# The MLP of two token blocks by Strassen's seven products, with the inner units through DRAM

## The chip, the cores and the metric

The kernel runs on one core of a Trainium2 chip. The metric is the device time of one execution in microseconds (us), the median of several runs. Engines: TensorE (PE; its weight loads are PEld), VectorE (DVE), ScalarE (ACT), GpSimd (POOL), and SyncE (SP), whose queue issues every DMA of this kernel.

## The reference

`x` is 2048 tokens by 1024 channels, float32. A Conformer convolution module and a dense MLP each add to it:

```python
h = rms_norm(x, mix_norm)
a, g = split(h @ w_in + b_in)                # 1024 -> 2 x 1024
h = causal_depthwise_conv31(a * sigmoid(g)) + conv_b
x = x + (silu(layer_norm(h)) @ w_out + b_out)
x = x + square(relu(rms_norm(x, mlp_norm) @ mlp_w1)) @ mlp_w2   # 1024 -> 4096 -> 1024
```

## The kernel before

Channels lie on the 128 partitions and tokens along the free axis, so x comes in transposed and the result leaves transposed. The tokens are cut into four blocks of T = 512 columns, one PSUM bank each; channels into KD = 8 chunks of 128, hidden units into 32 chunks, taken in NG = 8 groups of G = 4.

A float32 product is made of three passes of float32r: each operand is split into `hi` (a ScalarE copy) and `lo` (a subtraction on VectorE or GpSimd) by `halves` (L84, L85), and hi*hi + hi*lo + lo*hi is accumulated in PSUM by `mm` (L143). So a 128x128 block of weights against 512 tokens is three matmuls, and every weight block and every moving tile is cast and subtracted once.

The program is written in Tile: the code gives the operations and the sizes of rotating buffers (`bufs`), and Tile puts in the waits. Each engine works through its own instructions in a fixed order. `spawn`, `poll` and `finish` weave a generator's steps (a norm) between the products: `mm` polls once per contraction step, and a task yields how many polls it waits (WAIT = 7 before a norm's first product, GAP = 9 before its second).

The order of the work: the first pointwise product and the gate for all blocks, with the depthwise convolution (31 steps of VectorE per chunk, L329) running beside the products of other blocks; blocks 0 and 1 are convolved and normalised on the chip, projected by `w_out` and taken through the MLP, while blocks 2 and 3 pass through DRAM (`spill`, `conv_out`) and are normalised by `ln_spilled`. Then, for blocks 2 and 3: `fetch` loads and splits the convolved tiles (`s`, `act`); `project` multiplies by `w_out`, adds the bias and x (L384) and collects squares for the norm; its `norm` scales and splits the result (L392, then `act`). `mlp` runs group 0 for block 2 alone and then for block 3 alone, and groups 1 to 7 for both. `mlp_up` makes four hidden chunks a group: 24 matmuls into a bank, relu (L407) and square (L409) on ScalarE, then a split into `hid`. `mlp_down` multiplies them by `w2` and adds each bank to the residual `x2`, kept in SBUF (L420); the last group's sums are stored to `outT`. Weights come as `raw` tiles of 128x1024 (two buffers) and are split into `w` (three). These last stages are:

```python
ss = [fetch(i) for i in range(2)]
a2, a, ta = project(2, ss[0])
b2, b, tb = project(3, ss[1])
finish(ta)
mlp(0, [2], [a2], [a], nc.gpsimd)
finish(tb)
mlp(0, [3], [b2], [b])
for g in range(1, NG):
    mlp(g, [2, 3], [a2, b2], [a, b])
```

## Time and profile before

| | |
|---|---|
| median of 3 runs | 1987.99 us (1987.82 to 1989.01) |
| profiled execution: span from the first to the last instruction | 1987.9 us |
| busy: TensorE, VectorE, ScalarE, GpSimd | 1955.0, 1369.3, 653.7, 373.9 us |
| matmuls | 8576 |
| of these 128x512, by moving tile and weights | 4800 `act` by `w`, 3456 `hid` by `w`, 192 `act` by `hid` |
| DMA | 190.83 MB, 96 GB/s over the span |

Busy time is the time in which an engine executes; an engine's row says nothing of why it is idle. The profiled execution gives no time outside its span, which is within 0.1 us of the median. Matmuls overlap their neighbours, so the mean of one (391 ns) is more than the step from one to the next.

### The profile page before, as it was taken

Reading aid. Unit: us, or ns where it says so; the run is one execution under the profiler, and the core shown is the slowest. Engines: PE = TensorE matmul, PEld = TensorE weight load, DVE = VectorE, ACT = ScalarE, POOL = GpSimd, SP = SyncE. Lnnn points to the kernel's source line nnn. Section 1 sums busy time; section 2 is a strip of 40 time slices with the busy share of each in tenths; the row PEclk is TensorE's granted clock in tenths of the full one; section 3 lists DMA queues with packets and bytes.
Section 4 is the critical chain, followed back from the end, with each engine's and each line's share of the span. In section 5 each row is a group of like instructions: output and inputs, shape, how many; then the busy total and the mean of one; then the engine's idle time right before and its main releaser. Section 6 shows DMA issues by size and latency. Waiting matters only on the chain.

```text
span 1987.9 us, 22177 instructions
## 1 busy us (share of the span) xinstructions
PE 1955.0 (98%) x8576; PEld 1606.3 (81%) x8576; DVE 1369.3 (69%) x1976; ACT 653.7 (33%) x960; POOL 373.9 (19%) x215
## 2 busy tenths in 40 slices
PE   7999999999999999999999999999999999999999
PEld 6888888888778878788888788878888888888887
DVE  7999999999999999789999863553223232322322
ACT  5223225243453333443222442433322313132230
POOL 2256322644445630000000002410000000000000
PEclk9999999999999999999999999999999999999999
DMA  6223321432224333552212484322111111111112
GB/s 199 64 85 111 98 77 65 143 102 96 85 81 130 124 107 117 194 183 96 66 66 72 142 276 153 118 85 85 43 53 43 53 50 46 53 43 53 43 53 85
DMA packets 69801, 190.83 MB, mean 96 GB/s; under 512 B 7872, under 2 KB 8000, under 8 KB 69696
## 3 DMA queue, kind: packets, MB, share of 16 engines
q1 hardware_dynamic: 69696, 189.43, 29.1%
q8 instruction: 67, 1.10, 0.2%
q14 instruction: 38, 0.31, 0.1%
HBM read 163.98 MB, written 25.41 MB: 95 GB/s over the span
## 4 chain that ended last, share of the span: by engine, by line
PE 55%; issue 3%; DVE 1%; ACT 1%; DMA 1%; POOL 0%; DVEq 0%; ACTq 0%
PE ps L143 54%; DMA conv<-s 1%; DVE xn L392 0%; DVE act L85 0%; ACT s L336 0%; PE lps L212 0%; DVE w L85 0%; ACT relu L407 0%; ACT sq L196 0%; POOL r L223 0%; ACT w L84 0%; PE lps L203 0%; POOL acc L192 0%; DVE c L364 0%; ACT hid L84 0%
## 5 line engine op out<-in xcount | busy, mean ns | idle before, releaser
L143 PE MATMUL ps<-act,w 128*128 128x512 f32 x4800 | 1104.6, 391 | 10.8 <-ACT w L84 8.4
L143 PEld LDWEIGHTS ps<-act,w 128*128 128x128 f32 x4800 | 902.5, 188 | 202.4 <-ACT w L84 8.4
L143 PE MATMUL ps<-hid,w 128*128 128x512 f32 x3456 | 799.6, 392 | 8.4 <-DVE hid L85 4.9
L143 PEld LDWEIGHTS ps<-hid,w 128*128 128x128 f32 x3456 | 650.8, 189 | 150.4 <-DVE hid L85 7.9
L84 ACT CAST w<-raw 128x1024 fp32r<-128x1024 f32 (+1 forms) x238 | 247.3, 1040 | 611.7 <-PE ps L143 579.3
L329 DVE SCALAR_TENSOR_TENSOR cacc<-hc,cw,cacc 128x512 f32<-128x512 f32 x464 | 324.6, 749 | 1.4
L420 DVE TENSOR_TENSOR h<-h,ps 128x512 f32<-128x512 f32 x256 | 174.6, 685 | 207.9 <-PE ps L143 205.8
L329 DVE SCALAR_TENSOR_TENSOR cacc<-h,cw,cacc 128x512 f32<-128x512 f32 x464 | 316.9, 749 | 0.0
L85 POOL TENSOR_TENSOR w<-raw,w 128x1024 fp32r<-128x1024 f32 x98 | 236.7, 2415 | 315.1 <-ACT w L84 300.0
L85 DVE TENSOR_TENSOR w<-raw,w 128x1024 fp32r<-128x1024 f32 (+1 forms) x140 | 171.0, 1223 | 170.5 <-ACT w L84 170.3
L407 ACT ACTIVATE relu<-ps 128x512 f32<-128x512 f32 x128 | 76.4, 597 | 370.8 <-PE ps L143 366.6
L85 DVE TENSOR_TENSOR hid<-s,hid 128x512 fp32r<-128x512 f32 x128 | 99.5, 778 | 127.5 <-ACT hid L84 127.2
L409 ACT ACTIVATE s<-relu 128x512 f32<-128x512 f32 x128 | 80.9, 632 | 1.2
L84 ACT CAST hid<-s 128x512 fp32r<-128x512 f32 x128 | 79.6, 622 | 3.7
L192 POOL TENSOR_TENSOR acc<-acc,hc 128x512 f32<-128x512 f32 x12 | 13.1, 1092 | 250.6 <-DVE hc L329 202.4
L192 POOL TENSOR_TENSOR acc<-acc,sq 128x512 f32<-128x512 f32 x36 | 50.1, 1391 | 37.7 <-ACT sq L196 37.0
L384 DVE SCALAR_TENSOR_TENSOR h<-ps,vec,xt 128x512 f32<-128x512 f32 x32 | 23.9, 748 | 42.5 <-PE ps L143 42.2
L303 ACT ACTIVATE sg<-ps,vec 128x512 f32<-128x512 f32 x24 | 16.5, 687 | 98.5 <-PE ps L143 98.5
L196 ACT ACTIVATE sq<-h 128x512 f32<-128x512 f32 x64 | 39.4, 626 | 19.5 <-DVE h L384 7.8
L143 PE MATMUL ps<-act,hid 128*128 128x512 f32 x192 | 45.0, 391 | 0.0
L143 PEld LDWEIGHTS ps<-act,hid 128*128 128x128 f32 x192 | 35.9, 188 | 7.4
L84 ACT CAST act<-xn 128x512 fp32r<-128x512 f32 x48 | 29.6, 621 | 36.6 <-DVE xn L392 23.5
(69 smaller groups left out, 558.4 us busy)
## 6 DMA issues: line engine op xcount, KB each, us to landing
raw<-in_w SPq DMA_DIRECT2D x176, 512.0 KB, 3.3
xt<-in_xT SPq DMA_DIRECT2D x64, 256.0 KB, 3.4
raw<-in_w_out SPq DMA_DIRECT2D x32, 512.0 KB, 3.9
raw<-in_w_in SPq DMA_DIRECT2D x30, 512.0 KB, 3.3
outT<-h SPq DMA_DIRECT2D x32, 256.0 KB, 2.9
spill<-hs SPq DMA_DIRECT2D x16, 271.0 KB, 2.3
hc<-spill SPq DMA_DIRECT2D x16, 271.0 KB, 2.8
h<-in_xT SPq DMA_DIRECT2D x16, 256.0 KB, 5.8
```

Of the source, the lines that this page charges most:

```text
L84: nc.scalar.copy(hl[:, 0, :], src)
L85: eng.tensor_sub(hl[:, 1, :], src, hl[:, 0, :].bitcast(F32))
L143: nc.tensor.matmul(ps, lhsT=w(k, a), rhs=x[:, b, :], start=k == 0 and i == 0, stop=k == len(xs) - 1 and i == 2,)
L192: eng.tensor_add(self.acc, self.acc, t)
L196: nc.scalar.activation(q, t, AF.Square)
L303: nc.scalar.activation(sg, pg, AF.Sigmoid, bias=v(V_BIN + KD + j))
L329: nc.vector.scalar_tensor_tensor(out, h[:, k : k + T], cw[:, j, k : k + 1], acc, ALU.mult, ALU.add)
L384: nc.vector.scalar_tensor_tensor(o, ps, v(V_BO + m), x_tile(m, b), ALU.add, ALU.add)
L407: nc.scalar.activation(r, ps, AF.Relu)
L409: nc.scalar.activation(s, r, AF.Square)
L420: nc.vector.tensor_add(x2[i][m], x2[i][m], ps)
```

## The change

The MLP of blocks 2 and 3 is computed as 2x2 block products by Strassen's algorithm in Winograd's form: seven products of half-sized blocks in place of eight, with sums of blocks before and after. Going up, the moving matrix is [B11 B12; B21 B22]: the columns are blocks 2 and 3, the rows the upper and lower four channel chunks. Its forms B11, B21, B22, T1 to T4 (four tiles each) are made once by `norm_first` and `norm_second`. A `Quad` is two hidden chunks for both blocks: `sums` makes S1 to S4 of its weights, seven products of 12 matmuls go to the banks x, y and z, some of them accumulating on one another after a copy of the bank was taken, and the four results are squared and kept. Their own forms (again B11, B21, B22, T1 to T4) are computed on GpSimd and stored to DRAM, `hid_d`. Going down, a unit is a group g of four hidden chunks and one half `o` of the output channels: `hidden` loads and splits the stored forms, `blocks` loads and combines `w2`, and each of the seven products is two tiles of 6 matmuls; the results are added to `acc`. The projected x goes to DRAM too (`x2d`) and is loaded for the norm and as the start of `acc`. The first EARLY = 5 quads do products P1 and P2 while block 3's norm is made, put them away in DRAM and resume. The tile pools of the first part are closed, and new ones lie over them; with `reuse_waits="tile"` a new tile waits for the old tiles under it. `w2` has another layout, so that `mlp_down` of blocks 0 and 1 loads it in runs of 256 columns. The core of the diff, blank lines left out:

```diff
+EARLY = 5
+N_WQ, N_LD, N_CC = 6, 5, 6
...
-    sb = pool("sb", bufs=1)
-    psp = pool("psp", bufs=5, space=PSUM)
-    psc = pool("psc", bufs=2, space=PSUM)
+    front = ctx.enter_context(ExitStack())
+    acts = sb = front.enter_context(tc.tile_pool(name="sb", bufs=1))
+    n_act, n_tmp = 2 * KD, 4
+    psp = front.enter_context(tc.tile_pool(name="psp", bufs=5, space=PSUM))
+    psc = front.enter_context(tc.tile_pool(name="psc", bufs=2, space=PSUM))
...
+    def load_w2(g, m, eng=nc.vector):
+        raw, hl = raw_w(), w_tile()
+        nc.sync.dma_start(raw.rearrange("p (s c) -> p s c", s=4), w2[g, m // 4][:, :, m // 2 % 2, :])
+        halves(hl, raw, eng)
+        def w(x, k, a):
+            at = (2 * x + k % 2) * 2 * P + k // 2 * P
+            return hl[:, a, at : at + P]
+        return w
...
-                w = load_w(w2[g, m // 2], eng)
+                w = load_w2(g, m, eng)
             for i, b in enumerate(blocks):
                 ps = bank()
-                mm(ps, lambda k, a: w(m % 2 * G + k, a), hid[i])
+                mm(ps, lambda k, a: w(m % 2, k, a), hid[i])
...
-    ss = [fetch(i) for i in range(2)]
-    a2, a, ta = project(2, ss[0])
-    b2, b, tb = project(3, ss[1])
+    front.close()
...
+    def reopened(name, stack, **k):
+        return stack.enter_context(tc.tile_pool(name=name, bufs=1, reuse_waits="tile", **k))
+    psp = reopened("psb", ctx, space=PSUM)
+    wts = reopened("wts", ctx)
+    forms = ctx.enter_context(ExitStack())
+    acts = reopened("acts", forms)
+    n_act, n_raw, n_tmp = 29, 2, 2
+    phase = ctx.enter_context(ExitStack())
+    sb = reopened("projection", phase)
+    def xbank():
+        return psp.tile([P, T], F32, name="px", tag="ps", bufs=3)
...
+    def w_split(src, eng):
+        hl = wts.tile([P, 2, T], F32R, name="wq", tag="wq", bufs=N_WQ)
+        nc.scalar.copy(hl[:, 0, :], src)
+        eng.tensor_sub(hl[:, 1, :], src, hl[:, 0, :].bitcast(F32))
+        return hl
+    def raw_wq(src):
+        t = sb.tile([P, 2 * T], F32, name="rawq", tag="rawq", bufs=n_raw)
+        nc.sync.dma_start(t, src)
+        return t
...
+    def product(ps, hl, xs, off=0, first=True):
+        n = len(xs)
+        for k, x in enumerate(xs):
+            for i, (a, b) in enumerate(((0, 0), (0, 1), (1, 0))):
+                nc.tensor.matmul(
+                    ps,
+                    lhsT=hl[:, a, off + k * P : off + (k + 1) * P],
+                    rhs=x[:, b, :],
+                    start=first and k == 0 and i == 0,
+                    stop=k == n - 1 and i == 2,
+                    skip_group_check=True,
+                )
+            poll()
...
+    def load_plain(src):
+        raw = raw_wq(src)
+        hl = [w_split(raw[:, h * T : (h + 1) * T], (nc.vector, nc.gpsimd)[h]) for h in range(2)]
+        return lambda k, a: hl[k // 4][:, a, k % 4 * P : (k % 4 + 1) * P]
+    def project_spilled(b, ss, norm):
+        st = Stats(False)
+        for m in range(KD):
+            w = load_plain(w_out[m])
+            ps = xbank()
+            mm(ps, w, ss)
+            xt = loaded(xT[m * P : (m + 1) * P, (b + 2) * T : (b + 3) * T], "xt")
+            o = out_tile()
+            nc.vector.scalar_tensor_tensor(o, ps, v(V_BO + m), xt, ALU.add, ALU.add)
+            nc.sync.dma_start(x2d[b][m], o)
+            st.add_square(m, o)
+        return spawn(norm(st))
+    def x_normed(b, m, rs, xn):
+        x = loaded(x2d[b][m], "x2")
+        nc.vector.scalar_tensor_tensor(xn, x, v(V_MLP + m), rs, ALU.mult, ALU.mult)
+        return xn
...
+    def norm_first(st):
+        rs = yield from st.rstd_later(WAIT, GAP)
+        for k in range(HK):
+            n0[k] = acts.tile([P, 2, T], F32, name="n0", tag="act", bufs=n_act)
+            for y in range(2):
+                form["B11" if y == 0 else "B21"][k] = act_split(x_normed(0, y * HK + k, rs, n0[k][:, y, :]))
+                yield 1
+    def norm_second(st):
+        rs = yield from st.rstd_later(WAIT, GAP)
+        for k in range(HK):
+            b12 = x_normed(1, k, rs, small(sb, "n1", 3))
+            b22 = x_normed(1, HK + k, rs, small(sb, "n1", 3))
+            b11, b21 = n0[k][:, 0, :], n0[k][:, 1, :]
+            t1 = small(sb, "t1", 1)
+            nc.vector.tensor_sub(t1, b12, b11)
+            t2 = small(sb, "t2", 1)
+            nc.vector.tensor_sub(t2, b22, t1)
+            form["T2"][k] = act_split(t2)
+            form["T1"][k] = act_split(t1, nc.gpsimd)
+            yield 1
+            nc.vector.tensor_sub(b12, b22, b12)
+            form["T3"][k] = act_split(b12)
+            form["B22"][k] = act_split(b22, nc.gpsimd)
+            nc.vector.tensor_sub(b21, b21, t2)
+            form["T4"][k] = act_split(b21)
+            yield 1
+    ss = [[act_split(loaded(conv_out[j][i], "s")) for j in range(KD)] for i in range(2)]
+    ta = project_spilled(0, ss[0], norm_first)
+    tb = project_spilled(1, ss[1], norm_second)
     finish(ta)
-    mlp(0, [2], [a2], [a], nc.gpsimd)
+    NQ = NF // 2
+    hid_d = [{n: dram.tile([P, T], F32, name=f"h{n}_{q}") for n in form} for q in range(NQ)]
+    def added(ps, t, out=None):
+        out = out_tile() if out is None else out
+        nc.vector.tensor_add(out, ps, t)
+        return out
+    def squared_relu(c, src=None):
+        nc.scalar.activation(c, c if src is None else src, AF.Relu)
+        nc.scalar.activation(c, c, AF.Square)
+        return c
+    class Quad:
+        def __init__(self, q):
+            self.q, self.early = q, False
+        def keep(self, n, t):
+            nc.sync.dma_start(hid_d[self.q][n], t)
+        def high(self):
+            self.a1 = raw_wq(w1[2 * self.q])
+            self.x = xbank()
+        def sums(self):
+            a2 = raw_wq(w1[2 * self.q + 1])
+            a11, a12, a21, self.a22 = self.a1[:, :T], self.a1[:, T:], a2[:, :T], a2[:, T:]
+            self.s1, self.s2 = small(sb, "s1", 1), small(sb, "s2", 1)
+            nc.vector.tensor_add(self.s1, a21, self.a22)
+            nc.vector.tensor_sub(self.s2, self.s1, a11)
+            nc.vector.tensor_sub(a21, a11, a21)
+            self.s3, self.s4 = a21, a12
+        def p1(self):
+            product(self.x, w_split(self.a1[:, :T], nc.vector), form["B11"])
+            self.c1 = small(wts, "p1", 2)
+            nc.scalar.copy(self.c1, self.x)
+        def p2(self):
+            y = ybank()
+            product(y, w_split(self.a1[:, T:], nc.vector), form["B21"])
+            self.c11 = squared_relu(added(y, self.c1))
+            self.keep("B11", self.c11)
+        def leave(self):
+            self.early = dram.tile([P, T], F32, name=f"p1_{self.q}")
+            nc.sync.dma_start(self.early, self.c1)
+        def resume(self):
+            self.high()
+            self.c1 = small(wts, "p1", 2)
+            nc.sync.dma_start(self.c1, self.early)
+            self.c11 = out_tile()
+            nc.sync.dma_start(self.c11, hid_d[self.q]["B11"])
+        def copied(self, ps, name):
+            t = small(sb, name, 2)
+            if self.early:
+                return added(ps, self.c1, t)
+            nc.scalar.copy(t, ps)
+            return t
+        def p6(self):
+            product(self.x, w_split(self.s2, nc.vector), form["T2"], first=bool(self.early))
+            self.u2 = self.copied(self.x, "u2")
+            nc.vector.tensor_sub(self.s4, self.s4, self.s2)
+        def p5(self):
+            self.z = zbank()
+            product(self.z, w_split(self.s1, nc.vector), form["T1"])
+            self.c5 = self.copied(self.z, "p5")
+        def p7(self):
+            product(self.x, w_split(self.s3, nc.vector), form["T3"], first=False)
+            self.c22 = squared_relu(added(self.x, self.c5))
+            self.keep("B22", self.c22)
+        def p3(self):
+            product(self.z, w_split(self.s4, nc.gpsimd), form["B22"], first=False)
+            self.c12 = squared_relu(added(self.z, self.u2))
+        def p4(self):
+            product(self.x, w_split(self.a22, nc.gpsimd), form["T4"], first=False)
+            if self.early:
+                c21 = squared_relu(added(self.x, self.c1))
+            else:
+                c21 = squared_relu(out_tile(), self.x)
+            self.keep("B21", c21)
+            c11, c12, c22 = self.c11, self.c12, self.c22
+            t1, t2, t4 = [small(sb, n, 1) for n in ("h1", "h2", "h4")]
+            nc.gpsimd.tensor_sub(t1, c12, c11)
+            nc.gpsimd.tensor_sub(t2, c22, t1)
+            nc.gpsimd.tensor_sub(c12, c22, c12)
+            nc.gpsimd.tensor_sub(t4, c21, t2)
+            for n, t in (("T1", t1), ("T2", t2), ("T3", c12), ("T4", t4)):
+                self.keep(n, t)
+    quads = [Quad(q) for q in range(NQ)]
+    for u in quads[:EARLY]:
+        u.high()
+        u.p1()
+        u.p2()
+        u.leave()
     finish(tb)
-    mlp(0, [3], [b2], [b])
-    for g in range(1, NG):
-        mlp(g, [2, 3], [a2, b2], [a, b])
+    phase.close()
+    sb, n_raw = reopened("first", phase), 4
+    last = None
+    for u in quads:
+        if u.early:
+            u.resume()
+            u.sums()
+        else:
+            u.high()
+            u.sums()
+            u.p1()
+        if last:
+            last.p3()
+        if not u.early:
+            u.p2()
+        u.p6()
+        if last:
+            last.p4()
+        u.p5()
+        u.p7()
+        last = u
+    last.p3()
+    last.p4()
+    phase.close()
+    sb = reopened("second", phase)
+    ORDER = (("A11", "B11"), ("A12", "B21"), ("S2", "T2"), ("S1", "T1"), ("S3", "T3"), ("S4", "B22"), ("A22", "T4"))
...
+    def hidden(g):
+        out = {}
+        for n in (b for _, b in ORDER):
+            out[n] = [act_split(loaded(hid_d[2 * g + k][n])) for k in range(2)]
+        return out
+    def blocks(g, o):
+        a11, a12, a21, a22 = [small(sb, "w2r", 8) for _ in range(4)]
+        for i, t in enumerate((a11, a12, a21, a22)):
+            nc.sync.dma_start(t.rearrange("p (q c) -> p q c", q=2), w2[g, o][:, i])
+        s1, s2 = small(sb, "s1", 1), small(sb, "s2", 1)
+        nc.gpsimd.tensor_add(s1, a21, a22)
+        nc.gpsimd.tensor_sub(s2, s1, a11)
+        out = {"A11": w_split(a11, nc.vector), "A12": w_split(a12, nc.vector)}
+        out["S2"] = w_split(s2, nc.vector)
+        out["S1"] = w_split(s1, nc.vector)
+        nc.vector.tensor_sub(a21, a11, a21)
+        out["S3"] = w_split(a21, nc.vector)
+        nc.vector.tensor_sub(a12, a12, s2)
+        out["S4"] = w_split(a12, nc.vector)
+        out["A22"] = w_split(a22, nc.gpsimd)
+        return out
+    def both(tiles, name, hs, w, first=True):
+        for i, ps in enumerate(tiles):
+            product(ps, w, hs, off=i * 2 * P, first=first)
+    h = hidden(0)
+    for g in range(NG):
+        for o in range(2):
+            if g == 0:
+                for b in range(2):
+                    for m in range(4 * o, 4 * o + 4, 2):
+                        t = acts.tile([P, 2, T], F32, name="acc", tag="act", bufs=n_act)
+                        for i in range(2):
+                            acc[b][m + i] = t[:, i, :]
+                            nc.sync.dma_start(acc[b][m + i], x2d[b][m + i])
+            ws = blocks(g, o)
+            px, py, pz = [[f() for _ in range(2)] for f in (xbank, ybank, zbank)]
+            both(px, "P1", h["B11"], ws["A11"])
+            p1 = [copied(t, "p1", wts) for t in px]
+            both(py, "P2", h["B21"], ws["A12"])
+            c = [added(t, p) for t, p in zip(py, p1)]
+            def add(x, n, ts):
+                for i, t in enumerate(ts):
+                    a = acc[n][4 * o + 2 * i + x]
+                    nc.gpsimd.tensor_add(a, a, t)
+            add(0, 0, c)
+            both(px, "P6", h["T2"], ws["S2"], first=False)
+            u2 = [copied(t, "u2") for t in px]
+            both(pz, "P5", h["T1"], ws["S1"])
+            p5 = [copied(t, "p5") for t in pz]
+            both(px, "P7", h["T3"], ws["S3"], first=False)
+            add(1, 1, [added(t, p) for t, p in zip(px, p5)])
+            both(pz, "P3", h["B22"], ws["S4"], first=False)
+            add(0, 1, [added(t, p) for t, p in zip(pz, u2)])
+            both(px, "P4", h["T4"], ws["A22"], first=False)
+            for i, t in enumerate(px):
+                a = acc[0][4 * o + 2 * i + 1]
+                nc.vector.tensor_add(a, a, t)
+            if g == NG - 1:
+                for m in range(4 * o, 4 * o + 4):
+                    for b in range(2):
+                        nc.sync.dma_start(outT[m * P : (m + 1) * P, (b + 2) * T : (b + 3) * T], acc[b][m])
+            if o == 0 and g < NG - 1:
+                nxt = hidden(g + 1)
+        h = nxt
...
-        "w2": _tiles(a["mlp_w2"][0], G, 2),
+        "w2": np.ascontiguousarray(
+            a["mlp_w2"][0].reshape(NG, 2, 2, P, 2, 2, 2, P).transpose(0, 4, 3, 6, 2, 5, 1, 7)
+        ).reshape(NG, 2, P, 4, 2, 2 * P),
```

## Rows read from the trace of the kernel before

**Rows 1.** The page's table of engines: busy us, share of the span, instructions.
```profile
PE 1955.0 (98%) x8576; PEld 1606.3 (81%) x8576; DVE 1369.3 (69%) x1976; ACT 653.7 (33%) x960; POOL 373.9 (19%) x215
```

**Rows 2.** The chain that ended last, from 1280 us: start us, us, what.
```profile
1308.61 674.99 PE ps L143 x2963
...
1983.62 0.69 DVE h L420
```

**Rows 3.** Stretches: length, each engine's busy us (instructions), TensorE's clock, DMA share, GB/s.
```profile
1190.00:1234.00 44.00, 44.00 (x196) 36.44 (x195) 15.87 (x17) 12.22 (x16) 10.48 (x6) 1.00 0.54 172
...
1279.00:1308.00 29.00, 26.06 (x119) 21.31 (x117) 20.41 (x30) 14.70 (x24) 11.87 (x6) 1.00 0.25 84
1308.00:1374.00 66.00, 65.39 (x275) 53.53 (x276) 28.23 (x31) 20.67 (x28) 4.77 (x2) 0.95 0.29 96
...
1374.00:1940.00 566.00, 566.00 (x2499) 468.67 (x2498) 166.93 (x204) 150.79 (x217) 0.00 (x0) 1.00 0.15 49
```

**Rows 4.** Groups from 1374 to 1940 us: busy us, mean ns, idle before, releaser.
```profile
L420 DVE TENSOR_TENSOR h<-h,ps 128x512 f32<-128x512 f32 x97 | 66.7, 687 | 151.9 <-PE ps L143 151.9
...
L85 DVE TENSOR_TENSOR hid<-s,hid 128x512 fp32r<-128x512 f32 x55 | 38.1, 693 | 118.3 <-ACT hid L84 118.3
L409 ACT ACTIVATE s<-relu 128x512 f32<-128x512 f32 x55 | 34.8, 632 | 0.9
L84 ACT CAST hid<-s 128x512 fp32r<-128x512 f32 x55 | 34.3, 623 | 1.8
L407 ACT ACTIVATE relu<-ps 128x512 f32<-128x512 f32 x55 | 32.9, 598 | 183.0 <-PE ps L143 183.0
```

**Rows 5.** Timeline, two runs of three VectorE sums: start us, us, what.
```profile
1186.54 1.88 DVE L420 TENSOR_TENSOR h<-h,ps 128x512 f32<-128x512 f32 x3
...
1303.17 1.88 DVE L85 TENSOR_TENSOR act<-xn,act 128x512 fp32r<-128x512 f32 x3
```

**Rows 6.** GpSimd instructions on `act` and `acc`: duration ns min/median/max.
```profile
L85 POOL TENSOR_TENSOR act<-xn,act x8: 1302/1745/1752, 188.8 to 203.0; 128x512 fp32r<-128x512 f32 x8
...
L192 POOL TENSOR_TENSOR acc<-acc,sq x36: 1281/1295/2152, 86.3 to 1282.5; 128x512 f32<-128x512 f32 x36
```

**Rows 7.** Timeline from 188 to 201 us, GpSimd, then VectorE.
```profile
188.76 6.86 POOL L85 TENSOR_TENSOR act<-xn,act 128x512 fp32r<-128x512 f32 x4 [7.06 <-ACT act L84]
...
188.61 2.44 DVE L272 SCALAR_TENSOR_TENSOR xn<-xt,vec,rstd 128x512 f32<-128x512 f32 x2
190.97 0.74 DVE L329 SCALAR_TENSOR_TENSOR cacc<-h,cw,cacc 128x512 f32<-128x512 f32 x1
...
193.34 2.82 DVE L272 SCALAR_TENSOR_TENSOR xn<-xt,vec,rstd 128x512 f32<-128x512 f32 x2
```

**Rows 8.** DMA: SP's issues of `s` (ns min/median/max), then us to landing.
```profile
L163 SPq DMA_DIRECT2D s<-conv x16: 319/382/496, 848.2 to 1180.4; - x16
...
raw<-in_w SPq DMA_DIRECT2D x176, 512.0 KB, 3.3
...
outT<-h SPq DMA_DIRECT2D x32, 256.0 KB, 2.9
...
s<-conv SPq DMA_DIRECT2D x16, 256.0 KB, 4.4
```

**Rows 9.** Timeline from 1278 to 1312 us: the norm of block 3.
```profile
1278.93 0.75 DVE L384 SCALAR_TENSOR_TENSOR h<-ps,vec,xt 128x512 f32<-128x512 f32 x1 [4.69 <-PE ps L143]
...
1292.88 3.17 DVE L392 SCALAR_TENSOR_TENSOR xn<-h,vec,rstd 128x512 f32<-128x512 f32 x2 [1.69 <-ACT rstd L242]
...
1306.40 1.36 DVE L85 TENSOR_TENSOR act<-xn,act 128x512 fp32r<-128x512 f32 x2
...
1308.61 3.78 PE L143 MATMUL ps<-hid,w 128*128 128x512 f32 x8 [3.55 <-ACT hid L84]
```

**Rows 10.** Timeline from 1184 us: last split and first matmul of the projections.
```profile
1184.19 0.69 DVE L85 TENSOR_TENSOR act<-s,act 128x512 fp32r<-128x512 f32 x1 [1.70 <-ACT act L84]
...
1190.15 2.20 PE L143 MATMUL ps<-act,w 128*128 128x512 f32 x9
```

More of the change, by code (lines that the diff above doesn't have):

```diff
@@ L87, in act_tile @@
     def act_tile():
-        return sb.tile([P, 2, T], F32R, name="act", tag="act", bufs=2 * KD)
+        return acts.tile([P, 2, T], F32R, name="act", tag="act", bufs=n_act)
     def hid_tile():
@@ L370, in ln_spilled @@
             nc.sync.dma_start(conv_out[j][i], s)
-    def fetch(i):
-        return [act_split(stream("s", conv_out[j][i])) for j in range(KD)]
     def project(b, ss, eng=nc.vector):
@@ new lines, in conformer_mlp, with ybank, zbank @@
+    forms = ctx.enter_context(ExitStack())
[5 more added lines that the diff above has]
+        return psp.tile([P, T], F32, name="px", tag="ps", bufs=3)
+    def ybank():
+        return psp.tile([P, T], F32, name="py", tag="py", bufs=2)
+    def zbank():
+        return psp.tile([P, T], F32, name="pz", tag="pz", bufs=2)
+    def w_split(src, eng):
[3 more added lines that the diff above has]
+        return hl
@@ new lines, in conformer_mlp @@
+    x2d = [[dram.tile([P, T], F32, name=f"x2_{b}_{m}") for m in range(KD)] for b in range(2)]
+    def load_plain(src):
[14 more added lines that the diff above has]
+        return spawn(norm(st))
@@ new lines, in x_normed @@
+    def x_normed(b, m, rs, xn):
+        x = loaded(x2d[b][m], "x2")
+        nc.vector.scalar_tensor_tensor(xn, x, v(V_MLP + m), rs, ALU.mult, ALU.mult)
+        return xn
+    HK = KD // 2
+    form = {n: [None] * HK for n in ("B11", "B21", "B22", "T1", "T2", "T3", "T4")}
+    n0 = [None] * HK
+    def norm_first(st):
[5 more added lines that the diff above has]
+                yield 1
@@ new lines, in conformer_mlp, with copied @@
+    last.p3()
[3 more added lines that the diff above has]
+    ORDER = (("A11", "B11"), ("A12", "B21"), ("S2", "T2"), ("S1", "T1"), ("S3", "T3"), ("S4", "B22"), ("A22", "T4"))
+    acc = [[None] * KD for _ in range(2)]
+    def copied(ps, name, pool_=None):
+        t = small(pool_ or sb, name, 2)
+        nc.scalar.copy(t, ps)
+        return t
+    def hidden(g):
[3 more added lines that the diff above has]
+        return out
```

10 lines of the change are left out of this document (9 added, 1 removed).

## The prediction, before the changed kernel was run

> **What bounds the kernel now.** The page's table of engines comes first [rows 1]: TensorE is busy 98% of the span, VectorE 69%, ScalarE 33%, GpSimd 19%. An average over unlike stages decides little, so the next view is the chain of waits [rows 2]: from 1308.61 us to the end it is one piece of 674.99 us of matmuls, and after it a last sum on VectorE. The table by stretches [rows 3] then shows what stands beside the matmuls. From 1374 to 1940, thirteen of the alternating up and down halves of the MLP of blocks 2 and 3, TensorE is busy 566.00 of 566.00 us at a granted clock of 1.00 (its 2.4 GHz level), VectorE 166.93, GpSimd nothing. So in the part that is changed, TensorE alone sets the time, VectorE has some 70% to spare, and a matmul costs 566.00 / 2499 = 0.2265 us.
>
> **Removed.** Up, before: 32 hidden chunks x 8 channel chunks x 3 passes x 2 blocks = 1536 matmuls; down: 8 groups x 8 x 4 x 3 x 2 = 1536. After: 16 quads x 7 products x 4 chunks x 3 = 1344, and 16 units (8 groups x 2 values of `o`) x 7 x 2 tiles x 2 chunks x 3 = 1344. That is 384 fewer, of the same 128x512 shape and passes: 384 x 0.2265 = **-87.0 us**. A quad or a unit is 84 matmuls, 19.0 us. The Trainium skill (TensorE: Matmul & The Clock Gate, Back-to-back issue gap) gives 512 / 2.4 + 2.5 = 216 ns; by it the gain would be an estimated 83 us. The trace says 226.5 ns, and that decides.
>
> **Prices of what is added.** A VectorE sum over 512 columns lasts about 0.69 us in the table of groups [rows 4], but three in a row take 1.88 us, with one operand in PSUM as with both in SBUF [rows 5]: each next one costs (1.88 - 0.69) / 2 = 0.60 us. A ScalarE cast or copy is 0.62, relu 0.60, square 0.63 [rows 4]. A GpSimd sum or split is 1.30 alone (the lowest of `act`, `acc`) and up to 1.75 [rows 6]. Why, the timeline shows [rows 7]: between 188.76 and 195.62 four GpSimd splits take 6.86 us, 1.72 each, while VectorE's `xn` instructions, which read two tensors in SBUF, take 2.44 and 2.82 us for two; the convolution step at 190.97, with its other tensor in PSUM, takes its usual 0.74. GpSimd and a VectorE instruction with two SBUF inputs exclude each other; GpSimd holds VectorE up for about 1.72 - 0.66 = 1.05 us each. An instruction with an operand in PSUM goes on beside it.
>
> **The up half, per quad (19.0 us of TensorE).** VectorE: 3 in `sums`, 5 splits, 1 in `p6` (nine with two SBUF inputs) and 3 sums out of PSUM: 12 x 0.60 = 7.2 us. GpSimd: 2 splits and 4 sums of hidden units, 6 x 1.05 = 6.3. Even end to end that is 13.5. ScalarE: 7 casts, 3 copies, 8 for the squared relu, 18 x 0.62 = 11.2. DMA: two loads of 512 KB and seven stores of 256 KB, at some 0.35 us of SP's queue each [rows 8], 3 us; 2.8 MB in 19 us is 150 GB/s, where 172 GB/s went beside full matmuls [rows 3]. Each bank that a later product accumulates on must first be copied; two other products, 5.4 us, stand between. TensorE hides all of it; I put **+3 us** for 16 quads (0 to 16, a microsecond each).
>
> **The down half, per unit (19.0 us).** VectorE: 6 splits, 2 differences, 7 splits of hidden units (14 tiles a group, two units): 15 with two SBUF inputs, 9.0 us; 8 sums out of PSUM, 4.8. GpSimd: s1, s2, the split of A22, 6 sums into `acc`: 9 x 1.05 = 9.5. None of VectorE's 13.8 or GpSimd's 9.5 is above 19.0, but on the shared access to SBUF they add up: 9.0 + 9.5 = 18.5, nearly a unit, and if no GpSimd instruction finds VectorE at a PSUM sum, VectorE needs 13.8 + 9.5 = 23.3. So the ends are 19.0 (hidden) and 23.3. PSUM sums come in pairs, and the first one's GpSimd sum can run beside the second: 3 x 0.60 = 1.8 saved, some 0.8 more by chance, against 0.3 of waiting for casts and matmuls: I take 21.0, between the ends. What a held split delays is queued behind it on VectorE: the sums out of `px` after P7, which P4 must have before it accumulates on the same banks, three banks of 6 matmuls or some 4 us later; so short holds cost nothing and only the total counts. **16 x 2.0 = +32 us** (0 to 69). ScalarE (14 casts, 6 copies, 12.4 us) and DMA (5.7 MB a group of 38 us) have room.
>
> **The norm of block 3.** Before, its statistics come 14.0 us after the last projection product (1278.93 to 1292.88) and its 16 VectorE instructions run until 1307.8; TensorE then waits 3.55 us for a hidden unit [rows 9]. In 95 us there [rows 3] 394 matmuls ran where 419 fit: 5.7 us lost, 3.3 of them by the clock of 0.95 over 66 us after the wait. After, the same moment needs per chunk pair 2 normalised tiles (0.66 each) and 7 sums or splits on VectorE (5.5 us), and 2 GpSimd splits (2.1): 4 x 7.6 = 30.5 us, nearly serial, as `t1` and `t2` have one buffer. What covers it are the five early quads, 120 matmuls, 27.2 us. T2's last chunk comes some 4.7 us before the end: 14.0 + 30.5 - 4.7 = 39.8. TensorE can do 9 of P6's 12 matmuls before (2.0): it stands 10.6 us, and pays 3.3 for the clock. Less the 5.7 of before, **+8 us** (-6 if all is covered, +18 if `s2`, which lies where older statistics lay, waits for the end of the norm).
>
> **Seams and ends.** The new pools lie over old tiles. Before, blocks 2 and 3 have their inputs split 5 us ahead of their first matmul (1184.88 against 1190.15) [rows 10]; after, some of these tiles may lie over x2 of block 1, which is free only when its result is stored, 2.9 us after the last sum [rows 8], and then need a cast and a split, 1.2: **+3** (0 to 8). From up to down, a weight block must land (about 4.4, as `s` [rows 8]), be cast and split, but most of its room is free a quad earlier: **+3** (0 to 8). x2 and the hidden units' passage through DRAM is loads of this kind, ordered well ahead; no more for it. `w2` of blocks 0 and 1 comes in runs of 1 KB: a load lands in 3.3 us now [rows 8] and even at 5 two raw buffers give one each 4 us, under the 5.4 of 24 matmuls: 0. At the end two more stores queue: **+1.5** (0 to 3).
>
> **Sum.** -87.0 + 3 + 32 + 8 + 3 + 3 + 1.5 = -36.5. Against the profiled span of 1987.9 us (the runs' median is 1987.99, so nothing to add) that is **1951 us**. No measurement of this kernel tells less than about 0.2%, 4 us, from no change.
>
> **Rivals.** (a) *TensorE stays the bound in the down half*: the PSUM sums fall beside GpSimd's, 19.0 a unit, and the 32 us vanish: 1919 us. For it: VectorE at 13.8 of 19.0; against it: 18.5 of 19.0 of the shared access, in strict order. The Trainium skill (Perfetto Trace Analysis, Identifying the Most-Contended Engine) says that the engine with the highest occupancy limits a regime. By that rule TensorE limits and this case holds; rows 7 show a resource that no engine's occupancy counts.
> (b) *VectorE and GpSimd set the down half*: fully serial, 23.3, and TensorE, held at a bank whose sum is queued behind GpSimd, then lets VectorE wait six matmuls (1.4 us) once a unit: 24.7, 16 x 5.7 = 91 us, so 2010 us, slower. It decides from (87.0 - 18.5) / 16 = 4.3 above 19.0, at 23.3 a unit. For it: two buffers of `py` and `pz`, three of `px`, so little slack; against it: some overlap is certain, since sums into `acc` follow pairs.
> (c) *The passage through DRAM and the three reopened pools hold TensorE*: SP's one queue keeps loads behind stores that wait for GpSimd, a microsecond for each quad (+13 over the 3) and the upper ends at the seams and the norm (+20): 1984 us, no change. Against it: loads run a quad ahead.
> That the matmuls don't fall is excluded by the count.
>
> **Chances.** Forecast, 1930 to 1975: 0.48; (a) 0.26; (b) 0.14; (c) 0.12, half of it on the faster side. Faster 0.80, same 0.06, slower 0.14. The range of 1914 to 2000 takes in (a) and (c) and leaves out (b) and some below (a), under 2 in 10.
>
> **What would show it.** 8192 matmuls. Up quads at 19.0 us each with VectorE near half busy; down units at 21 us, VectorE over 85% busy, its two-SBUF splits well above their 0.69 us, GpSimd's sums at 1.7, TensorE waiting for sums out of PSUM in `px`. A gap near 11 us after the early quads. If down units run at 19.0, the exclusion was sized wrongly, (a); if up quads exceed 20, the order of the queues, (c). Wrong altogether if TensorE's step per matmul changes with groups of 6 or 12.

## The result, and the profile after

The changed kernel takes 2001.86 us (median of 4 runs, 2000.47 to 2002.29) where the kernel before took 1987.9: the ratio is 1.0071, with a 95% interval of 1.0056 to 1.0085. It is slower, by 14 us or 0.7%, where 37 us less was forecast, and it lies just above the range. The profiled execution has a span of 1999.6 us, 11.7 above that of before. Its own time is 2001.76, so 2.2 us lie outside the span; in every run here these are 1.7 to 2.2, the kernel before included (1986.61 us with a span of 1984.8). So that its profiled span equals its median suggests that the profiled execution was some 2 us longer than the median one. The account below is of the 11.7 us between the two spans.

The page's table of engines of the changed kernel (busy us, share of the span, instructions), which answers to [rows 1]:

```profile
PE 1883.3 (94%) x8192; PEld 1538.8 (77%) x8192; DVE 1640.7 (82%) x2315; ACT 820.4 (41%) x1322; POOL 751.3 (38%) x471
```

The 384 matmuls are gone and TensorE is busy 72 us less; so it must be idle longer. The table by stretches of the changed kernel, to be read beside [rows 3] (length, then each engine's busy us and instructions, granted clock, DMA share, GB/s), shows where:

```profile
1210.00:1304.00 94.00, 93.57 (x405) 77.24 (x406) 42.57 (x65) 37.78 (x63) 40.55 (x31) 0.97 0.66 223
1304.00:1355.00 51.00, 28.81 (x121) 23.09 (x119) 38.91 (x57) 22.68 (x41) 15.33 (x10) 0.81 0.40 136
1355.00:1420.00 65.00, 59.96 (x244) 48.56 (x245) 41.82 (x59) 26.00 (x44) 28.65 (x20) 0.91 0.57 194
1420.00:1640.00 220.00, 217.92 (x961) 180.14 (x960) 132.83 (x146) 122.13 (x218) 105.53 (x72) 1.00 0.48 159
1640.00:1670.00 30.00, 15.87 (x51) 12.22 (x51) 11.01 (x16) 13.21 (x24) 9.96 (x7) 0.67 0.76 257
1670.00:1950.00 280.00, 260.80 (x1127) 211.18 (x1126) 256.95 (x308) 152.48 (x267) 191.25 (x121) 0.99 0.46 144
```

The steady part of the up half (1420 to 1640) is full. Two short stretches are half empty: the norm of block 3 (1304 to 1355) and the passage from up to down (from 1640). In these two stretches the granted clock averages 0.81 and 0.67, a mix of the 1.2 and the 2.4 GHz level. The down half is 7% empty. What TensorE waits for, from 1180 us on (us in total, times, longest):

```profile
PE px L586 <- ACT wq L561: 24.9, 2, 14.1
PE px L163 <- ACT wq L561: 22.8, 1, 22.8
PE px L586 <- DVE acc L864: 18.7, 14, 2.9
PE py L586 <- DVE cc L665: 13.7, 1, 13.7
```

Four long waits make 61.4 us: 22.8 ahead of the projections, 13.7 and 10.8 in the norm, 14.1 ahead of the down half. The 14 short ones are the down half's. They stand behind the last VectorE sums of a unit, those after P4 (L864), which free the `px` banks for the next unit. The prediction had expected waits for sums out of `px`, but for those after P7, inside the unit.

**Where the time went.** With 0.2265 us a matmul, by the starts of the stages in the timelines:

| stretch | lost or saved, us |
|---|---|
| first projection product at 1210.43, before at 1190.15 | +20.3 |
| projections, 1210.43 to 1301.69, for 384 matmuls | +4.3 |
| early quads, norm, up half, seam: 1301.69 to 1660.52, 1344 matmuls | +54.4 |
| down half, 1660.52 to 1994.78, 1344 matmuls | +29.9 |
| after the last product: 4.8, before 4.3 | +0.5 |
| lost in these places before: 1190.15 to 1983.62, less 3456 matmuls | -10.7 |
| 384 matmuls | -87.0 |
| sum | +11.7 |

**The front seam.** The timeline of the changed kernel, SP's issues and the first weights:

```profile
1161.76 26.92 SPq L439 DMA_DIRECT2D outT<-h  x11
...
1188.72 14.63 SPq L575 DMA_DIRECT2D s<-conv  x16
1203.41 0.42 SPq L567 DMA_DIRECT2D rawq<-in_w_out  x1
...
1209.76 1.14 ACT L561 CAST wq<-rawq 128x512 fp32r<-128x512 f32 x2 [2.18 <-DMA rawq<-in_w_out]
...
1210.43 5.87 PE L163 MATMUL px<-act,wq 128*128 128x512 f32 x13 [22.84 <-ACT wq L561]
```

SP works through its issues in order. Until 1188.7 it stands at the last eleven stores of blocks 0 and 1, which wait for VectorE's sums (ten waits, 22.5 us); then sixteen `s` loads pass through five buffers at the pace of the splits (eleven waits, 6.8 us); only then come the first weights. Before, `s` was issued by 1180.4 [rows 8] and split by 1184.88 [rows 10], while TensorE was still at the last products of blocks 0 and 1.

**The norm of block 3.** Its timeline, the second product of early quad 2, VectorE's `t1` of the later chunk pairs, the sum of that early quad, what TensorE does behind it, and quad 0's weights:

```profile
1315.59 1.42 DVE L618 SCALAR_TENSOR_TENSOR n<-x,vec,rstd 128x512 f32<-128x512 f32 x2 [0.52 <-ACT rstd L262]
...
1316.75 2.88 PE L586 MATMUL py<-act,wq 128*128 128x512 f32 x12
...
1322.31 1.78 DVE L641 TENSOR_TENSOR t<-n,n 128x512 f32<-128x512 f32 x1
...
1330.03 1.75 DVE L641 TENSOR_TENSOR t<-n,n 128x512 f32<-128x512 f32 x1
...
1337.70 1.74 DVE L641 TENSOR_TENSOR t<-n,n 128x512 f32<-128x512 f32 x1
...
1340.64 0.68 DVE L665 TENSOR_TENSOR cc<-py,p 128x512 f32<-128x512 f32 x1
...
1341.46 5.02 PE L586 MATMUL py<-act,wq 128*128 128x512 f32 x12 [13.66 <-DVE cc L665]
...
1350.39 0.87 SPq L567 DMA_DIRECT2D rawq<-in_w  x2
...
1355.15 0.69 DVE L690 TENSOR_TENSOR s<-rawq 128x512 f32<-128x512 f32 x1 [6.67 <-DMA rawq<-in_w]
...
1357.27 3.23 PE L586 MATMUL px<-act,wq 128*128 128x512 f32 x6 [10.80 <-ACT wq L561]
```

The statistics come 13.9 us after the projections' end (1301.69), and a chunk pair takes 7.7 us: the forecast had 14.0 and 7.6. But the sums out of `py` of early quads 2, 3 and 4 stand behind the norm in VectorE's order. Quad 2's product is done at 1319.6 and its sum starts at 1340.64; as there are two `py` banks, the last of the ten early products waits 13.7 us for it. The twelve matmuls behind this wait take 5.02 us, where twelve took 2.88 before it. When they are through, quad 0's weights are not there: their tiles are in the next pool.

**From up to down.** The same, at the next pool:

```profile
1650.10 1.26 POOL L756 TENSOR_TENSOR h<-cc,h 128x512 f32<-128x512 f32 x1
...
1651.39 0.32 SPq L680 DMA_DIRECT2D hT<-h  x1
...
1653.44 1.84 SPq L812 DMA_DIRECT2D w2r<-in_w  x4
...
1659.85 1.26 ACT L561 CAST wq<-w2r 128x512 fp32r<-128x512 f32 x2 [2.83 <-DMA w2r<-in_w]
...
1660.52 3.78 PE L586 MATMUL px<-act,wq 128*128 128x512 f32 x8 [14.13 <-ACT wq L561]
```

`w2` is issued behind the last quad's stores, which wait for GpSimd's sums; it arrives 6 us later.

### The profile page after: what moved, and what is told of

Read it like the earlier page. It is cut to its first block, busy times and chain, and to the rows that moved or that the text cites. A ratio compares the mean times of both kernels' runs of the same rounds, so it can differ in the third digit from the quotient of the medians.

```text
span 1999.6 us, 23532 instructions
## 1 busy us (share of the span) xinstructions
PE 1883.3 (94%) x8192; PEld 1538.8 (77%) x8192; DVE 1640.7 (82%) x2315; ACT 820.4 (41%) x1322; POOL 751.3 (38%) x471
## 4 chain that ended last, share of the span: by engine, by line
PE 40%; DVE 8%; issue 5%; DMA 4%; POOL 2%; ACT 1%; SPq 0%; POOLq 0%; DVEq 0%; ACTq 0%
PE ps L163 16%; PE px L586 11%; PE pz L586 5%; PE px L163 5%; PE py L586 3%; DVE act L93 2%; DVE wq L562 2%; DVE cc L665 1%; DMA rawq<-in_w 1%; DMA w2r<-in_w 1%; POOL s L814 1%; DVE acc L864 1%; ACT act L92 0%; POOL wq L562 0%; DMA s<-conv 0%
## 5 line engine op out<-in xcount | busy, mean ns | idle before, releaser
L163 PE MATMUL ps<-act,w 128*128 128x512 f32 x2880 | 666.2, 391 | 10.3 <-ACT w L92 7.9
L163 PEld LDWEIGHTS ps<-act,w 128*128 128x128 f32 x2880 | 541.4, 188 | 126.8 <-ACT w L92 7.9
L163 PE MATMUL ps<-hid,w 128*128 128x512 f32 x1920 | 445.6, 392 | 4.8 <-DVE hid L93 4.4
L163 PEld LDWEIGHTS ps<-hid,w 128*128 128x128 f32 x1920 | 360.0, 188 | 85.3 <-DVE hid L93 7.2
L586 PE MATMUL px<-act,wq 128*128 128x512 f32 x1536 | 375.5, 397 | 48.0 <-ACT wq L561 24.9
L586 PEld LDWEIGHTS px<-act,wq 128*128 128x128 f32 x1536 | 291.8, 191 | 116.8 <-ACT wq L561 25.8
L586 PE MATMUL pz<-act,wq 128*128 128x512 f32 x768 | 186.3, 392 | 2.1 <-ACT p L722 2.1
L850 POOL TENSOR_TENSOR acc<-acc,cc 128x512 f32<-128x512 f32 x96 | 149.5, 1575 | 89.1 <-DVE cc L665 77.2
L586 PEld LDWEIGHTS pz<-act,wq 128*128 128x128 f32 x768 | 145.4, 189 | 33.0 <-ACT p L722 2.5
L93 DVE TENSOR_TENSOR act<-ld,act 128x512 fp32r<-128x512 f32 x112 | 106.2, 971 | 15.8 <-ACT act L92 15.3
L163 PE MATMUL px<-act,wq 128*128 128x512 f32 x384 | 90.5, 398 | 22.8 <-ACT wq L561 22.8
L586 PE MATMUL py<-act,wq 128*128 128x512 f32 x384 | 95.3, 398 | 13.7 <-DVE cc L665 13.7
L163 PEld LDWEIGHTS px<-act,wq 128*128 128x128 f32 x384 | 73.8, 193 | 39.0 <-ACT wq L561 23.3
```

The source lines that it names most:

```text
L93: eng.tensor_sub(hl[:, 1, :], src, hl[:, 0, :].bitcast(F32))
L163: nc.tensor.matmul(ps, lhsT=w(k, a), rhs=x[:, b, :], start=k == 0 and i == 0, stop=k == len(xs) - 1 and i == 2,)
L586: nc.tensor.matmul(ps, lhsT=hl[:, a, off + k * P : off + (k + 1) * P], rhs=x[:, b, :], start=first and k == 0 and i == 0, stop=k == n - 1 ...
L850: nc.gpsimd.tensor_add(a, a, t)
```

## The experiments

Unless another number is given, each kernel here ran once. The kernel before, run beside them, took 1985.04 to 1991.08 us, so differences of a few us between them tell nothing. "Less" and "more" are against the changed kernel's 2001.86 us where no other run is named.

**The stores' queue alone.** The stores of blocks 0 and 1 leave through GpSimd's queue:

```diff
-                    nc.sync.dma_start(outT[m * P : (m + 1) * P, b * T : (b + 1) * T], x2[i][m])
+                    nc.gpsimd.dma_start(outT[m * P : (m + 1) * P, b * T : (b + 1) * T], x2[i][m])
```

> The 16 stores of the result of blocks 0 and 1 are issued from GpSimd's queue in place of SP's; nothing else is changed. In the changed kernel TensorE stands 23.2 us between the last product of block 1 and the first of the projections. Seam theory (the loads for the new pools stand on SP's queue behind stores that wait for sums): the loads of s start some 20 us earlier, the gap falls from 23.2 to under 8 us, and the span from 1999.6 to about 1982. Tile theory (the loads wait for the old tiles that lie under the new ones): the gap stays over 15 us and the span over 1992.

1999.86 us, beside 1986.61 for the kernel before; no change at the seam, where TensorE waits 23.1 us. Its timeline:

```profile
1164.95 43.21 SPq L575 DMA_DIRECT2D s<-conv  x16
1197.52 2.70 ACT L92 CAST act<-s 128x512 fp32r<-128x512 f32 x5 [32.97 <-DMA outT<-h]
...
1208.21 0.42 SPq L567 DMA_DIRECT2D rawq<-in_w_out  x1
...
1214.24 2.08 PE L163 MATMUL px<-act,wq 128*128 128x512 f32 x4 [23.14 <-ACT wq L561]
```

`s` is issued 24 us earlier, but its cast waits for the last store, whose tile lies under the new `act` tile; and the weights still come behind sixteen `s`. Three things stand in a row here, and taking this one away alone gains nothing.

**The order of the loads alone.** Two weight blocks ahead of `s`:

```diff
+    ahead = [load_plain(w_out[m]) for m in range(2)]
     ss = [[act_split(loaded(conv_out[j][i], "s")) for j in range(KD)] for i in range(2)]
-    ta = project_spilled(0, ss[0], norm_first)
+    ta = project_spilled(0, ss[0], norm_first, ahead)
```

> The changed kernel with one edit: the first two weight blocks of the projection are loaded ahead of the sixteen s loads; stores, pools and all else as they were. In the changed kernel SP's queue ends the stores of block 1 at 1188.7 us, issues s until 1203.35, and only then the weights, which TensorE has at 1210.4. Theory, the order of the loads is the larger part of the 23 us at the seam: weights split by about 1194, the first eight s tiles by about 1197 to 1200, so the gap falls to 10 to 14 us and the time to 1986 to 1993 us. Rival, the tiles of block 1 that lie under the new act tiles are the larger part: s is split no earlier than 1205, the gap stays above 18 us and the time above 1995 us.

1991.95 us: 10 less. The weights are no longer the last to come; in the waits of this run the wait of 22.8 has become

```profile
PE px L163 <- ACT act L92: 9.3, 1, 9.3
```

So the order of SP's own loads was over half of the wait. The rest is less sure: here the stores hold SP until 1195.2, and with the stores moved as well, in the last two kernels below, 7.9 and 7.8 us remain; in the first of them the cast of `s` comes behind the last store's landing.

**One pool for the three phases.** Projection, up and down share one pool and its tags, so nothing is closed between them; to fit, small buffers share slots and their numbers change (`t1` and `t2` of the norm get two each, for one):

```diff
-    n_act, n_raw, n_tmp = 29, 2, 2
+    n_act, n_raw, n_tmp = 29, 4, 2
...
-    phase.close()
-    sb, n_raw = reopened("first", phase), 4
...
-    phase.close()
-    sb = reopened("second", phase)
```

> The projection, up and down phases share one pool with four raw buffers, in place of three pools that are closed and opened again; small buffers share slots. Seam theory: the 11.2 us gap ahead of quad 0 and the 14.5 us gap between the up and the down half go down to under 4 us each, and the span from 1999.6 to about 1975. Data theory (TensorE waits there for the norm's last forms and for the last quads' hidden units): both gaps stay within 4 us of what they were, and the span above 1993.

1985.65 us, 16 less. TensorE's wait ahead of quad 0 falls from 10.8 to 0.4 us and the one of 14.1 ahead of the down half goes; the front seam stays (23.0) and so does the early quads' wait, and one in the last quad grows from 2.1:

```profile
PE py L586 <- DVE cc L665: 13.9, 1, 13.9
PE pz L586 <- ACT p L722: 5.5, 1, 5.5
```

So the two pool seams cost what they showed, 24.5 us. But the down half, in this pool, takes 8.8 us more, 343.1 for 334.3: most of its units alternate 19.04 with 23.7 to 25.2. Which of the changed buffers does that was not tried.

**GpSimd's sums into `acc`, 8 columns of 512:**

```diff
-                    nc.gpsimd.tensor_add(a, a, t)
+                    nc.gpsimd.tensor_add(a[:, :8], a[:, :8], t[:, :8])
```

> Leaves out work: GpSimd's sums into acc cover 8 of their 512 columns. Contention theory (GpSimd and VectorE exclude each other on SBUF): with six of nine GpSimd instructions short, a steady unit of the down half falls from 20.46 us (mean of 21.1 and 19.83) to 19.2 or less, some 20 us in all. Order theory (the sums out of px stand too late in VectorE's order, or three px banks are too few): a unit stays above 20.2 us.

1979.44 us, 22 less; after the first three, a down unit is 19.0 to 19.2. But this kernel leaves work out, and says nothing of who held whom. The next run does.

**All of GpSimd's work of the down half on VectorE** (six sums into `acc`, S1, S2, the split of A22):

```diff
-                    nc.gpsimd.tensor_add(a, a, t)
+                    nc.vector.tensor_add(a, a, t)
...
-        nc.gpsimd.tensor_add(s1, a21, a22)
-        nc.gpsimd.tensor_sub(s2, s1, a11)
+        nc.vector.tensor_add(s1, a21, a22)
+        nc.vector.tensor_sub(s2, s1, a11)
...
-        out["A22"] = w_split(a22, nc.gpsimd)
+        out["A22"] = w_split(a22, nc.vector)
```

> All GpSimd work of the down half (two sums of weights, the split of A22, six sums into acc) is done by VectorE: 32 instructions a unit of about 0.60 us, 19.2 us, against 23 and 13.8 before. Contention theory: since a GpSimd instruction holds VectorE up for 1.05 us where VectorE needs 0.60 for it, a unit falls from 20.46 to 19.3 to 19.9 us. If the two do not exclude each other: VectorE goes from 13.8 to 19.2 us of work plus its waits, and a unit rises to 21 us or more.

1978.47 us, 23 less, though VectorE has 32 instructions a unit in place of 23. Groups from 1700 to 1930 us, first of the changed kernel (busy us, mean ns of one, idle before and its releasers):

```profile
L850 POOL TENSOR_TENSOR acc<-acc,cc 128x512 f32<-128x512 f32 x68 | 108.1, 1608 | 64.5 <-DVE cc L665 57.1 <-DMA acc<-x 6.7 <-PE px L586 0.7
L93 DVE TENSOR_TENSOR act<-ld,act 128x512 fp32r<-128x512 f32 x77 | 73.5, 976 | 1.5 <-ACT act L92 1.5
L562 DVE TENSOR_TENSOR wq<-w2r,wq 128x512 fp32r<-128x512 f32 x44 | 59.1, 1352 | 1.1 <-ACT wq L561 1.1
```

then of this run:

```profile
L93 DVE TENSOR_TENSOR act<-ld,act 128x512 fp32r<-128x512 f32 x84 | 54.7, 685 | 0.9 <-ACT act L92 0.5
L850 DVE TENSOR_TENSOR acc<-acc,cc 128x512 f32<-128x512 f32 x72 | 46.2, 683 | 0.0
L562 DVE TENSOR_TENSOR wq<-w2r,wq 128x512 fp32r<-128x512 f32 x58 | 38.3, 685 | 0.0
```

The same split takes 1352 ns beside GpSimd and 685 without it. A sum that GpSimd makes in 1608 ns, holding VectorE up, VectorE makes in 683. Every unit is 19.0 to 20.6 us.

**The early quads' sums ahead of the norm.** Tile's priority around one sum:

```diff
-            self.c11 = squared_relu(added(y, self.c1))
+            with tc.high_priority():
+                c = added(y, self.c1)
+            self.c11 = squared_relu(c)
```

> In the early quads the sum out of the bank py is put ahead of the norm's instructions in VectorE's order; nothing else is changed. Order theory (quad 3's second product waits 14.05 us for a bank because quad 1's sum is queued behind the norm's burst on VectorE): that gap falls under 3 us and the early quads end some 13 us sooner; the gap ahead of quad 0 grows, since the norm itself (30 us of VectorE and GpSimd) ends no sooner, so the two gaps together fall from 25.2 us to between 14 and 22. Throughput theory (VectorE is simply full): both gaps together stay within 2 us of 25.2.

1991.58 us, 10 less. The wait of 13.7 us goes, but the one ahead of quad 0 grows from 10.8 to 20.9: the five quads are used up at 1330.1 and the norm and quad 0's sums, in VectorE's order, last to 1351. Five quads of P1 and P2, 27 us, don't cover the norm.

**Both mends of the front seam, one pool, and a new order of the pools** (the phase's pool ahead of `acts`, to lie over other old tiles), on top of the first three edits above:

```diff
-    acts = reopened("acts", forms)
...
-    sb = reopened("projection", phase)
+    sb = reopened("projection", ctx)
+    acts = reopened("acts", ctx)
```

> As e2, and for the first seam: the pool of the phases lies below the pool of the forms, so that the first act tiles lie over tiles that are free early; the stores of blocks 0 and 1 go through GpSimd's queue; two weight tiles of w_out are loaded ahead of the 16 s tiles. Seam theory (queue order, old tiles and the order of the loads are three locks on one gap, so that e1 opened one and saw nothing): the 23.4 us gap ahead of the projections falls under 5 us, and the span from e2's 1983.9 to about 1960. If the gap has another cause, such as the layer norm of block 3 ending late, it stays over 12 us.

1993.02 us, 7 more than with one pool alone, where some 24 less was expected, although the seam's wait is 11.8 in place of 23.0. A unit without any wait takes 19.60 us, not 19.04: TensorE's step itself has grown.

**All mends, with five and with eight early quads.** The run above with the early sums first and the down half on VectorE:

> e6 with e5's order and with e4's down half on VectorE. If the three causes (seams, order in the norm, exclusion) are separate and add up: e6's span less about 20 us for the down half and 5 to 10 for the norm, some 1930 us. If what one frees is lost to another, above 1945.

1972.30 us, not the 1930 that three separate causes would give. Then

```diff
-EARLY = 5
+EARLY = 8
```

> e7 with eight early quads in place of five, 43.5 us of matmuls beside the norm in place of 27.2. Cover theory (the norm takes VectorE about 44 us from the end of the projections, and only products that don't need it can stand there): the gap ahead of quad 0 falls by 12 to 16 us against e7 and the span to about 1915. If the gap comes from the raw weights' loads or the sums of quad 0, it stays within 4 us of e7.

1972.05 us: no difference, where 12 to 16 less was expected. The wait of 12.0 us ahead of quad 0 becomes 5.5 and some small ones, but now eight quads resume with sums on VectorE, and TensorE waits for them six times up to 1463, 7.8 us in all: moved, not won. Both still have the longer step.

**The order of the pools alone, on the run with one pool:**

```diff
-    acts = reopened("acts", forms)
...
-    sb = reopened("projection", phase)
+    sb = reopened("projection", ctx)
+    acts = reopened("acts", ctx)
```

> The run with one pool for the three phases, and of the further edits only the order of the pools: the pool of the phase is opened ahead of acts. The instructions are the same. Theory, placement sets the step: 0.2333 us, a unit without waits 19.60 us, so some 20 us above the 1985.65 of the run with one pool, less what the seam may give back (0 to 11): 1994 to 2006 us. Rival: the step stays at 0.2267, and the time at 1975 to 1987 us.

1998.24 us, 12.6 more than with one pool. Stretches of the up half in which TensorE never stops, first of the run with one pool in the old order:

```profile
1450.00:1600.00 150.00, 150.00 (x663) 124.20 (x662) 88.52 (x97) 81.08 (x142) 71.77 (x49) 1.00 0.48 154
```

and of this run:

```profile
1450.00:1600.00 150.00, 150.00 (x644) 120.91 (x643) 69.33 (x95) 81.07 (x138) 60.30 (x47) 1.00 0.44 152
```

663 matmuls or 644 in 150 us, at the same granted clock: 226.2 or 232.9 ns a step. The changed kernel, too, has 663. Each engine works through the same instructions in the same order in the two runs: what the edit changes is where the tiles lie. VectorE and GpSimd are busy less in this layout (69.33 against 88.52 us, 60.30 against 71.77), so it isn't more work of theirs that slows TensorE.

**All mends in the old order of the pools** (`EARLY = 8`, both mends of the seam, one pool, early sums first, the down half on VectorE). Against the run with eight early quads:

```diff
-    sb = reopened("projection", ctx)
-    acts = reopened("acts", ctx)
+    acts = reopened("acts", forms)
...
+    sb = reopened("projection", phase)
```

> This kernel carries all the mends of the run with eight early quads, but leaves the new pools in the order of the changed kernel (wts, acts, the pool of the phase) where that run had the phase's pool ahead of acts. Theory, the step of a matmul hangs on where the tiles lie: the step goes back from 0.2333 to 0.2267 us, a quad or a unit of 84 matmuls from 19.60 to 19.04 us, and 3072 x 0.0066 = 20 us come back; the upper end of the front seam may be some us longer: 1950 to 1958 us. Rival, the step rose through the stores on GpSimd's queue or the weights loaded ahead: it stays at 0.2333 and the time at 1970 to 1976 us.

1961.99 us (4 runs, 1957.08 to 1965.33), a ratio of 0.9858 to the kernel before (0.9834 to 0.9883): faster than both. The step is back at 0.227 us, but of the 20 us expected 10 came (13, if each is taken against the kernel before that ran beside it). In the down half a unit takes 20.2 us on average where it took 20.3 with the longer step. VectorE is near its limit there, but something else holds it too. The stretch from 1700 to 1930, first of the run that only moved the down half's GpSimd work to VectorE, then of this one, and a wait of VectorE in this one:

```profile
1700.00:1930.00 230.00, 228.26 (x1000) 187.08 (x999) 227.75 (x377) 127.64 (x233) 0.00 (x0) 1.00 0.45 145
...
1700.00:1930.00 230.00, 222.78 (x957) 179.05 (x957) 220.53 (x364) 125.60 (x230) 0.00 (x0) 0.99 0.42 134
...
DVE act L93 <- ACT act L92: 11.1, 13, 2.5
```

With the same work on VectorE, the three pools let 1000 matmuls pass and this kernel 957. Here VectorE waits 11.1 us (1640 to 1950) for casts of the stored hidden tiles, which wait for their loads; there (1670 to 1950) it waited 0.5. So the one pool, which had lengthened the down half by itself, is the likely cause; the down half in its own pool, with the other mends, was not tried.

**S1 and S2 back on GpSimd, in that kernel:**

```diff
-        nc.vector.tensor_add(s1, a21, a22)
-        nc.vector.tensor_sub(s2, s1, a11)
+        nc.gpsimd.tensor_add(s1, a21, a22)
+        nc.gpsimd.tensor_sub(s2, s1, a11)
```

> The run with all mends and the old order of the pools, where VectorE is busy 291 of 310 us of the down half (a unit takes 20.3 us on average), with two of a unit's nine moved sums, S1 and S2 of w2, put back on GpSimd. Theory, TensorE waits for VectorE's count and for S1 and S2 that stand in VectorE's order behind other work: 30 x 0.605 + at most 2 x 1.05 of exclusion = 18.2 to 20.3 us a unit, so 19.3 on average, 16 us less over 16 units and 1943 to 1953 us. Rival, the exclusion charges its full price wherever GpSimd works, 1.05 against 0.60 us: a unit grows by 2 x 0.45 = 0.9 us, and the time to 1970 to 1978 us.

1961.27 us (4 runs, 1958.80 to 1965.67), ratio 0.9874 (0.9858 to 0.9891): no difference, and neither price was right. Its stretch:

```profile
1700.00:1930.00 230.00, 224.54 (x979) 182.40 (x978) 220.26 (x344) 126.43 (x227) 31.17 (x22) 1.00 0.41 136
```

With 22 sums on GpSimd VectorE does 344 instructions in place of 364 and is busy as long, while 2% more matmuls pass. From 1640 to 1950 it is 449 instructions in place of 477, 291.33 against 291.19 us, with 0.6% more matmuls (1296 and 1288). So a sum given to GpSimd costs VectorE most of what doing it costs.

## Why the prediction was wrong

**Right.** The removed matmuls: 150.00 / 663 = 0.2262 us a step in the full stretch, 86.9 us for 384 against 87.0. The up half outside its ends: no loss from 1450 to 1600. The mechanism of the down half: GpSimd holds VectorE up, and the two runs that take GpSimd's work away or move it show it. Its size, +29.9 us against +32, is in part luck: the first three units, behind the seam, average 23.3 us and the other thirteen 20.3, where every unit was put at 21.0; and TensorE waits for the sums after P4 and not for those after P7. VectorE's splits beside GpSimd at up to twice their length were foreseen from [rows 7]. The Trainium skill (SBUF — State Buffer, Who interferes with whom) has it that the pair of ports that the two engines share is an exclusive lock, and that a VectorE instruction with two inputs in SBUF contends with a GpSimd instruction that reads SBUF; this case agrees, with 1352 against 685 ns.

**The step that failed: "Seams and ends" and the cover of the norm.** The front seam was put at +3, "0 to 8". It cost 20.3, and the projections ran 4.3 us over, their start at the lower clock among that. The estimate took a store's landing, a cast and a split, the latency of one tile, and not the order of the queue: eleven stores that wait for sums, then sixteen loads through five buffers, then the weights. The program showed all three, the text named SP's queue as a lock at the seams only in rival (c), and the argument there, that loads run a quad ahead, holds inside a phase but not across a closed pool. The same holds for up to down: +3 forecast, a wait of 14.1 us measured, which one pool takes away. The seam between them, from the projection's pool to the first half's, ahead of quad 0, had no term at all: 10.8 us, which one pool also takes away.

**The norm** was put at +8 (13.9 with what it lost before). Its length was right: 13.9 us for the statistics, 7.7 for a chunk pair. What failed was "what covers it are the five early quads": the sums of three of them stood behind the norm on VectorE, whose order the text worked out for the down half and not here. Putting these sums first moves most of the wait to quad 0, so the cover was also too short. That `t1` and `t2` have one buffer was not what mattered: with two each, in the run with one pool, the wait was 13.9 us. The bound of +18, for `s2` late, was the nearer in number, but for another cause. Early quads, norm and both ends of the up half lost 54.4 us where 13.9 + 3 + 3 = 19.9 were counted.

These terms make the miss: seam 17.3 and projections 4.3, up half with its norm and end 34.5, together 56.1 us; -2.1 of the down half, -1.0 of the end and -5.0 that the kernel before lost beyond what was counted leave 48.

**The rivals.** (a), TensorE the bound at 19.0 a unit, fell. The rule of the Trainium skill named beside it (Perfetto Trace Analysis, Identifying the Most-Contended Engine) judges TensorE by its useful arithmetic and its weight loads, not by its busy matmuls. From 1670 to 1950 the weight loads were busy 211.18 of 280 us and VectorE 256.95 (the matmuls 260.80), so by the weight loads the rule names VectorE, where the prediction had it name TensorE. Even so, moving work onto VectorE made the kernel faster, as part of its busy time was being held by GpSimd. (b), 2010 us, is near the time and wrong in its cause: 20.9 us a unit on average, not 24.7. (c) named the place, SP's loads behind stores at reopened pools, but its +20 for the seams and the norm was too little, and its 13 us inside the up half didn't occur.

**What stays open.** Why the step of a matmul depends on the order of the pools; which tile it is was not tried, and the place of the tiles changes the timing of VectorE and GpSimd as well. In the best two kernels 7.9 us of the front seam, the norm and the small waits behind it, the passage to the down half (5.9 and 5.5 us), and a down half of 20.2 us a unit remain; each was seen in the trace, none taken away.

## What to carry to other kernels

Price a seam by the queue and the engine order, not by a latency: write down what stands ahead of the first load of the new phase on its queue, what that waits for, and which old tile lies under the new one; what is left of them sets what is left of the wait. Work that is to cover a wait must not need the engine that is waited for: check its place in that engine's order. Before giving VectorE's work on SBUF to GpSimd, count what GpSimd holds up.

## What was not expected of the hardware

The step from one 128x512 matmul to the next was 226.2 ns with the pools in one order and 232.9 with another, at a granted clock of 1.00 and with the same instructions; over the 3072 matmuls from the projections to the end that would be 20 us, and the run with nothing else changed was 12.6 us longer. And a sum in SBUF on GpSimd cost VectorE most of what VectorE would have taken for it: 449 instructions in place of 477 left it 291.33 against 291.19 us busy, for 0.6% more work.
